# A two-layer hybrid encoder on one core: where the squares are added, when the norm sums run, and the order of the convolution steps

## The chip, the core and the metric

The kernel runs on one core of one Trainium2 chip. The metric is the device time of one execution in microseconds (us). Engines are named as the profile names them: PE (TensorE; PEld are its weight loads), DVE (VectorE), ACT (ScalarE), POOL (GpSimd) and SP (SyncE, which only issues transfers here). "L564" is line 564 of the kernel before.

## The reference, cut to what matters

Two sequences (512 and 256 tokens, together T = 768 columns) go through two layers of width 1024. All arithmetic is float32.

```
for l in range(DEPTH):
    xn = rmsnorm(x, norm1_g[l])
    z = xn @ w_in[l]
    o_a = mixer_a(...)   # gelu, layernorm, spatial gating
    o_b = mixer_b(...)   # banded attention with a sink and a relative bias
    o_c = mixer_c(...)   # q and k: RMS norm, gain, 2-D rotary; full attention
    merged = sum over the mixers of sigmoid(xn @ w_gate + b_gate) * (o @ w_branch)
    x = x + merged @ w_out[l]
    x = x + conv_ffn(rmsnorm(x, norm2_g[l]), w_up[l], conv_w[l], conv_b[l], w_down[l])
return rmsnorm(x, final_g)

def conv_ffn(x, w_up, cw, cb, w_down):
    h = x @ w_up
    hp = jnp.pad(h, ((0, 0), (1, 1), (0, 0)))
    h = hp[:, :-2] * cw[0] + hp[:, 1:-1] * cw[1] + hp[:, 2:] * cw[2] + cb
    gt, val = jnp.split(h, 2, axis=-1)
    return (jax.nn.silu(gt) * val) @ w_down
```

## The kernel before

Activations lie transposed: eight tiles of 128 channels by 768 tokens. Every float32 product is three matmuls, of a high and a low half: wh*xh, wh*xl, wl*xh. ACT makes a weight's high half `wh` (L327, L337), and DVE the low half `wl` (`flush`, L357); DVE or ACT take the results out of PSUM. The program gives each engine its instructions in the order in which they are written; nothing reorders them, so an instruction that waits holds up everything behind it on its engine. A `plan()` lists the weights in order of use. At most three pairs of halves are held, and the next 512 KB weight is loaded by SP only when `flush` has read the raw tile of an earlier one.

**First norm.** The start of the program makes the halves of the eight input tiles (L1275 to L1278, L489, L490) and squares each tile on ACT (`sumsq`, L499). The first product (`dense_tok`, mixer A, L564) runs at the same time, on inputs not yet normed. The squares are added into two sums: tiles 2 to 5 by a POOL-issued transfer that accumulates in SBUF (L508), tiles 6 and 7 and the two sums by DVE (L504, L506). In the middle of the second half of that product PE sums over the channels (`rstd_tok`, L514); then DVE (L517) and POOL (a power of -0.5, L520) make the factor that ACT applies as it empties PSUM (L596).

**Mixer C's tables.** `cs` (cosines and sines) and the gains are fetched by POOL-issued transfers (L880, L885); the gain transfers repeat 64 numbers over 128 partitions and six blocks. DVE multiplies them into `tab` (L888). The product for k and v of mixer C follows (`dense_tok`, L564), then the generator `qknorm`, which uses `tab` (L903).

**FFN.** `layer_out` ends with the last of eight output projections; its squares are summed like those of the start. Then w_up comes in seven pieces for each of 22 groups g, 12 matmuls of 384 columns each, in the order P1, P4 of g-1, P2, P3 of g-1, P6, P5, P7 (the first group: P1, P2, P6, P5, P7). After (0, P5) come `rstd_tok` and `rstd_diag` (DVE L530, ACT L531, DVE L532), after (1, P1) `rstd_bc` (PE L544, ACT L546), whose result scales h in `scaled` (L1066). The transfers `sum1` to `sum4` (POOL, L275) prepare weights for the pieces; each is issued at the start of a piece.

After P4 the value half, after P3 the gate half of a group goes through steps that `later(n, f)` sets n ticks ahead. A piece gives two ticks, a down projection one per k (three or four). `CHAIN` gives the ticks: scaled, centre (ACT, L1058), taps (two DVE instructions, L1062 and L1063), and for the gate half silu (ACT, L1086), the product (DVE, L1089), high half (ACT, L1095), low half (DVE, L1101). The last group uses `CHAIN_END`. The buffer h of group g is written again by group g+2 (first by ACT, L1129, at the end of its P1). Down projections (L435) of a finished chunk lie between the pieces and after them; each fills one of two PSUM tiles `d`, and DVE adds it to x (L1180), or in the last chunk of the last layer (L1170).

Of the kernel before, what the change touches and what calls it, by code (L numbers as in the profile page):

```python
# [13 lines left out]
ALU = mybir.AluOpType  # L14
# [6 lines left out]
KD = D // P  # L21
# [4 lines left out]
HD = 64  # L26
# [4 lines left out]
D_FF = 2816  # L31
NJ = D_FF // P
FFC = [(0, 3), (3, 3), (6, 3), (9, 3), (12, 3), (15, 3), (18, 4)]
CHAIN = (2, 4, 6, 9, 11, 13, 15)
CHAIN_END = (1, 2, 3, 5, 6, 7, 8)
TAIL = 5
HT = T // 2
HW = T + 3
# [36 lines left out]
def ffn_steps(l):  # L75
# [14 lines left out]
    for g, p in seq:  # L90
# [4 lines left out]
        if p == "P3" and ends.get(g, last) < last:  # L95
            ready.append((t + CHAIN[-1] + 2, ends[g]))
        while ready and ready[0][0] <= t:
# [32 lines left out]
def encoder_kernel(ctx, tc, x_d, w_d, vec_d, ln_d, rope_d, gqk_d, oneh_d, relb_d, mask_d, id_d, y_d):  # L130
    nc = tc.nc
    PE, ACT, DVE, POOL = nc.tensor, nc.scalar, nc.vector, nc.gpsimd
# [19 lines left out]
    def page(w=T, dt=F32):  # L152
        return pp.tile([P, w], dt, tag="pg", name=nm("pg"))
# [243 lines left out]
    def start_bg(gen, rate):  # L397
        bg.append((gen, rate))
# [10 lines left out]
    def finish_bg(n=0):  # L409
        while len(bg) > n:  # L410
            if next(bg[0][0], "end") == "end":
                bg.pop(0)
# [38 lines left out]
    st = {}  # L451
# [39 lines left out]
        if k is not None:  # L491
            sumsq(x_ap, k, new=lambda: unit(F32)[:, 0])

    def sumsq(x_ap, k, dve=False, new=None):

        n = x_ap.shape[-1]
        c = 0 if dve else k % 2
        sq = (new or page)()[:, 0:n]
        ACT.activation(sq, x_ap, AF.Square)  # L499
        if k == c:  # L500
            st["acc", c] = sq
            return
        if dve or k >= KD - 2:
            DVE.tensor_tensor(st["acc", 0], st["acc", 0], sq, ALU.add)  # L504
            if not dve and k == KD - 2:
                DVE.tensor_tensor(st["acc", 0], st["acc", 0], st.pop(("acc", 1)), ALU.add)  # L506
        else:
            POOL.dma_start(out=st["acc", c], in_=sq, accum_op=ALU.add)  # L508
# [69 lines left out]
    def layer_mixers(l, xs):  # L578
# [299 lines left out]
        cs = page()  # L878
        for g in range(2):
            POOL.dma_start(out=cs[:, g * 384:(g + 1) * 384], in_=rope_d[g])  # L880
        tab = []
        for g in range(2):
            gt = page()
            for s in range(2):
                POOL.dma_start(  # L885
                    out=gt[:, s * 384:(s + 1) * 384],
                    in_=bass.AP(gqk_d.tensor, gqk_d.offset + ((l * 2 + g) * 2 + s) * HD, [[0, P], [0, NT], [1, HD]]))
            DVE.scalar_tensor_tensor(gt, cs, -(HD ** -0.5) if g == 0 else 1.0, gt, ALU.mult, ALU.mult)  # L888
            tab.append(gt)

        def qknorm(z, nh, tb, cats, dst):
# [65 lines left out]

        dense_tok(("in2", l, 1792 + 512, 0), ("in2", l, 1792 + 512, 1), xs, evac_kv)
        finish_bg()
        start_bg(qknorm(zk, 2, tab[1], "k", kc), BG_N)  # L960
        for c in range(2):
            z = flat(unit(F32))
# [75 lines left out]
    def layer_ffn(l, xs2, x_mid, x_spill):  # L1038
# [14 lines left out]
        def cw(i, ct):  # L1053
            return vec[:, VCW + i * 44 + ct:VCW + i * 44 + ct + 1]
# [3 lines left out]
            ACT.activation(f, h[:, 1:770], AF.Identity, scale=cw(1, ct), bias=vec[:, VCB + ct:VCB + ct + 1])  # L1058
            return f

        def taps(f, h, ct):
            DVE.scalar_tensor_tensor(f, h[:, 0:769], cw(0, ct), f, ALU.mult, ALU.add)  # L1062
            DVE.scalar_tensor_tensor(f, h[:, 2:771], cw(2, ct), f, ALU.mult, ALU.add)  # L1063

        def scaled(h):
            DVE.tensor_tensor(h[:, 1:770], h[:, 1:770], st["bcg"][:, 1:770], ALU.mult)  # L1066

        def conv_v(g):
            s = G[g]
            hv = s["h"][:, 1]  # L1070

            def c():
                s["fv"] = centre(hv, NJ + g)
            for n, f in zip(CHAIN_END if g == NJ - 1 else CHAIN,
                            (lambda: scaled(hv), c, lambda: taps(s["fv"], hv, NJ + g))):
                later(n, f)

        def conv_g(g):
            s = G[g]
            hg = s["h"][:, 0]  # L1080

            def c():
                s["fg"] = centre(hg, g)

            def si():
                ACT.activation(s["fg"], s["fg"], AF.Silu)  # L1086

            def mu():
                DVE.tensor_tensor(s["fg"], s["fg"], s["fv"], ALU.mult)  # L1089

            def hi():
                u = unit()
                f = s["fg"]
                for a, b, o in ((0, 512, 0), (512, 768, 1)):
                    ACT.activation(u[:, 0, a:b], f[:, a + o:b + o], AF.Copy)  # L1095
                s["u"] = u

            def lo():
                u, f = s["u"], s["fg"]
                for a, b, o in ((0, 512, 0), (512, 768, 1)):  # L1100
                    DVE.tensor_tensor(u[:, 1, a:b], f[:, a + o:b + o], fl(u[:, 0, a:b]), ALU.subtract)  # L1101
                hs[g] = u
                del G[g]
            for n, f in zip(CHAIN_END if g == NJ - 1 else CHAIN,
                            (lambda: scaled(hg), c, lambda: taps(s["fg"], hg, g), si, mu, hi, lo)):
                later(n, f)

        RIGHT = ((1 + HT, 513, 0, 512 - HT), (514, 770, 512 - HT, HT))
# [55 lines left out]
        def evac(c, m, cuts, ps):  # L1164
            last = c == len(FFC) - 1
            final_ = last and l == DEPTH - 1
            if final_:
                t0, t1 = cuts
                xa = st["xu"][m // 2][:, m % 2, t0:t1]
                DVE.tensor_tensor(xa, ps[:, 0, 0:t1 - t0], xa, ALU.add)  # L1170
                sumsq(xa, m, dve=True)
                if t0 and m == 2:
                    finish_bg()
                if m == KD - 1:
                    start_bg(final(st["xu"], t0, t1), 1.0)
                    if t0:
                        finish_bg()
                return
            xa = D.pop((c, m))
            DVE.tensor_tensor(h2(xa), ps[:, :, 0:384], h2(xa), ALU.add)  # L1180
            nc.sync.dma_start(out=(x_spill if last else x_mid)[m], in_=xa)
            if last:
                u = unit()
                prep(xa, st["vec"][:, VN1 + m:VN1 + m + 1], u, m)
                xs_next.append(u)
# [5 lines left out]
        for s in steps:  # L1191
            if s[0] == "pc":
                piece(s[1], s[2])
                if (s[1], s[2]) == (0, "P5"):
                    rstd_tok()
                    rstd_diag()
                elif (s[1], s[2]) == (1, "P1"):
                    rstd_bc(gap=True)
                elif s[1] == NJ - 1 and s[2] == "P3":
                    deep = 3  # L1200
                    if l < DEPTH - 1:
                        load_vec(l + 1)
                    else:
                        st["xu"] = [unit(F32) for _ in range(4)]
                continue
            _, c, m, cuts = s
            j0, nj = FFC[c]
            last = c == len(FFC) - 1
            final_ = last and l == DEPTH - 1
            for _, c2, m2, cuts2 in downs[0:deep]:  # L1210
                if not (c2 == len(FFC) - 1 and l == DEPTH - 1):
                    fetch(c2, m2)
                elif cuts2[0] == 0:
                    fetch_last(m2)
            downs.pop(0)
            while any(j not in hs for j in range(j0, j0 + nj)):
                tick()
            if cuts[0] == 0:
                hi, lo = W.get(("down", l, c, m))
                if final_:  # L1220
                    kept[m] = hi, lo
            else:
                hi, lo = kept[m]
            ps = dps()
            dense(ps, hi, lo, 0, [(w, j0 + k) for w, k in kidx(nj)], hs, True, True, cuts=cuts)
            evac(c, m, cuts, ps)
            if m == KD - 1 and not (final_ and cuts[0] == 0):
                for j in range(j0, j0 + nj):
                    del hs[j]
# [24 lines left out]
    with tc.manual_schedule():  # L1254
# [3 lines left out]
        xu = [unit(F32) for _ in range(4)]  # L1258
# [13 lines left out]
        for k in range(KD):  # L1272
            u = unit()
            if k < 4:
                ACT.activation(u[:, 0], xu[k // 2][:, k % 2], AF.Identity, scale=st["vec"][:, VN1 + k:VN1 + k + 1])  # L1275
                parts[k][0]()
                parts[k][1]()
                DVE.scalar_tensor_tensor(u[:, 1], xu[k // 2][:, k % 2], st["vec"][:, VN1 + k:VN1 + k + 1], fl(u[:, 0]),  # L1278
                                         ALU.mult, ALU.subtract)
            else:  # L1280
                prep(xu[k // 2][:, k % 2], st["vec"][:, VN1 + k:VN1 + k + 1], u, None)
            xs.append(u)
            if k == 3:
                W.load()
            if k == 5:
                W.split()
                W.flush()
            if k > 2:
                sumsq(xu[(k - 3) // 2][:, (k - 3) % 2], k - 3)
        for k in range(KD - 3, KD):  # L1290
            sumsq(xu[k // 2][:, k % 2], k)
        del u, xu
        spill = [dram.tile([P, T], F32, name=f"sp{k}") for k in range(KD)]
        x_mid = [dram.tile([P, T], F32, name=f"xm{k}") for k in range(KD)]
# [135 lines left out]
```

## Time and profile before

| | |
|---|---|
| time, median of 3 runs | 2453.21 us (2449.05 to 2453.59) |
| profiled execution | 2457.03 us, span 2455.3 us |
| busy PE / DVE / ACT / POOL | 2388.1 / 1523.8 / 1110.0 / 260.3 us |
| mean granted TensorE clock | 0.989 |
| HBM traffic | 243.93 MB read, 52.43 MB written |

The span runs from the first to the last instruction of the profiled execution; its own time is 1.7 us longer. A row of waits names who ended an engine's idle time, with the sum in us, how often, and the longest. A row of the timeline has its start, its duration, the engine, line and operation, and in brackets the engine's idle time before it and what ended that. Releasers are inferred: where two things ended at once, the row may name the wrong one.

### The profile page before, as it was taken

What the parts mean: (1) busy time and instruction counts of PE and PEld (TensorE: products, weight loads), DVE (VectorE), ACT (ScalarE), POOL (GpSimd) and SP (SyncE); (2) the same over time, 40 slices, a digit from 0 to 9 for tenths busy, and PEclk for the clock granted to TensorE, in tenths of its full rate; (3) what the DMA queues carried; (4) which work ended last, traced back from release to release, by engine and by line L of the source; (5) the groups of instructions that cost most, each with busy time, mean ns of one, the idle gap of its engine ahead of it and who ended that gap; (6) DMA issues with size and microseconds to landing.
All of it is one profiled execution on the core that took longest, in us unless ns stands there. A gap on an engine that the chain in (4) does not pass through costs nothing.

```text
span 2455.3 us, 38491 instructions
## 1 busy us (share of the span) xinstructions
PE 2388.1 (97%) x14990; PEld 2315.9 (94%) x14990; DVE 1523.8 (62%) x2656; ACT 1110.0 (45%) x2184; POOL 260.3 (11%) x390
## 2 busy tenths in 40 slices
PE   7999999999999999999999999999999999999997
PEld 7998999889989999999999999998899899999996
DVE  4555535554558777777645554555445687777785
ACT  4344434662345444444433443456424554444452
POOL 1000110000122111111000000100001211111100
PEclk8999999999999999999999999999999999999998
DMA  5511231012467888887732113210135688888854
GB/s 159 108 52 57 52 64 61 27 35 73 137 161 173 244 225 231 230 228 209 219 108 62 57 50 63 61 45 34 44 102 161 145 221 230 228 230 227 227 160 147
DMA packets 134950, 328.24 MB, mean 134 GB/s; under 512 B 15976, under 2 KB 29416, under 8 KB 134768
## 3 DMA queue, kind: packets, MB, share of 16 engines
q1 hardware_dynamic: 101232, 251.83, 31.6%
q0 software_dynamic: 33536, 73.95, 17.0%
q8 instruction: 118, 1.93, 0.3%
q14 instruction: 64, 0.52, 0.1%
HBM read 243.93 MB, written 52.43 MB: 121 GB/s over the span
## 4 chain that ended last, share of the span: by engine, by line
PE 85%; DMA 5%; DVE 4%; ACT 3%; issue 2%; POOL 0%; SPq 0%; POOLq 0%; DVEq 0%; ACTq 0%
PE d L435 47%; PE ga L1121 12%; PE gb L1121 9%; PE d L564 8%; PE s L809 3%; PE s L796 2%; PE s L757 2%; DMA qc<-w_pk 2%; DMA pg<-gqk 1%; DVE wl L357 1%; PE s L669 1%; ACT wh L327 1%; DMA qd<-qc 1%; DMA raw<-w_pk 1%; DMA pg<-pg 0%
## 5 line engine op out<-in xcount | busy, mean ns | idle before, releaser
L435 PE MATMUL d<-u,wh 128*128 128x384 f32 x4480 | 990.1, 343 | 6.8 <-ACT pg L1086 6.3
L435 PEld LDWEIGHTS d<-u,wh 128*128 128x128 f32 x4480 | 782.6, 189 | 21.8 <-issue 11.0
L435 PE MATMUL d<-u,wl 128*128 128x384 f32 x2240 | 575.3, 338 | 0.0
L435 PEld LDWEIGHTS d<-u,wl 128*128 128x128 f32 x2240 | 408.0, 188 | 0.0
L357 DVE TENSOR_TENSOR wl<-raw,wh 128x512 fp32r<-128x512 f32 (+1 forms) x261 | 248.4, 953 | 232.5 <-ACT wh L337 180.8
L1121 PE MATMUL ga<-u,wh 128*128 128x384 f32 x1408 | 364.5, 340 | 7.6 <-ACT u L1129 4.4
L1121 PE MATMUL gb<-u,wh 128*128 128x384 f32 x1056 | 271.0, 338 | 1.9 <-DVE u L1131 1.9
L1121 PEld LDWEIGHTS ga<-u,wh 128*128 128x128 f32 x1408 | 257.1, 189 | 9.5 <-ACT u L1129 5.0
L564 PE MATMUL d<-wh,u 128*128 128x256 f32 x1344 | 248.3, 285 | 3.0 <-ACT u L596 1.9
L1121 PE MATMUL ga<-u,wl 128*128 128x384 f32 x704 | 238.7, 339 | 0.0
L564 PEld LDWEIGHTS d<-wh,u 128*128 128x128 f32 x1344 | 210.9, 191 | 5.2 <-ACT u L596 3.1
L564 PE MATMUL d<-wl,u 128*128 128x256 f32 x672 | 190.7, 284 | 4.9 <-DVE wl L357 4.8
L1121 PEld LDWEIGHTS gb<-u,wh 128*128 128x128 f32 x1056 | 191.6, 188 | 2.7 <-ACT wh L327 1.8
L337 ACT ACTIVATE wh<-raw 128x1024 fp32r<-128x1024 f32 x129 | 135.3, 1049 | 104.3 <-PE d L564 44.9
L1121 PE MATMUL gb<-u,wl 128*128 128x384 f32 x528 | 178.0, 337 | 0.0
L1058 ACT ACTIVATE pg<-u,vec 128x769 f32<-128x769 f32 x88 | 91.0, 1034 | 124.5 <-DVE u L1066 82.0
L1180 DVE TENSOR_TENSOR pg<-d,pg 128x768 f32<-128x768 f32 x104 | 99.5, 956 | 76.5 <-PE d L435 76.0
L564 PEld LDWEIGHTS d<-wl,u 128*128 128x128 f32 x672 | 128.6, 191 | 5.5 <-DVE wl L357 5.2
L1121 PEld LDWEIGHTS ga<-u,wl 128*128 128x128 f32 x704 | 133.2, 189 | 0.0
L662 DVE TENSOR_TENSOR u<-s,u 128x128 fp32r<-128x128 f32 (+1 forms) x112 | 36.9, 329 | 114.5 <-ACT u L661 114.3
L757 PE MATMUL s<-u,u 128*128 128x256 f32 (+2 forms) x384 | 99.9, 342 | 2.2 <-ACT pg L797 1.6
L768 ACT ACTIVATE pg<-pg,sm 128x257 f32<-128x257 f32 (+1 forms) x96 | 52.5, 547 | 109.1 <-DVE sm L766 104.7
(204 smaller groups left out, 3190.1 us busy)
## 6 DMA issues: line engine op xcount, KB each, us to landing
raw<-w_pk SPq DMA_DIRECT2D x174, 512.0 KB, 3.7
pg<-xm SPq DMA_DIRECT2D x104, 384.0 KB, 4.6
xm<-pg SPq DMA_DIRECT2D x96, 384.0 KB, 3.4
u<-w_pk SPq DMA_DIRECT2D x96, 192.0 KB, 3.6
qa<-w_pk SPq DMA_DIRECT2D x44, 256.0 KB, 3.8
qb<-w_pk SPq DMA_DIRECT2D x44, 256.0 KB, 3.2
qc<-w_pk SPq DMA_DIRECT2D x44, 256.0 KB, 3.2
qd<-w_pk SPq DMA_DIRECT2D x44, 256.0 KB, 3.5
```

The costliest lines, as they stand in the source:

```text
L337: ACT.activation(hi[:, :n], t[:, :n], AF.Copy)
L357: DVE.tensor_tensor(lo, t, fl(hi), ALU.subtract)
L435: PE.matmul(out=ps[:, h, 0:b - a], lhsT=w, rhs=x[:, a:b], start=first and i == 0 and pi == 0, stop=last and i == nk - 1 and pi == 2,)
L564: PE.matmul(out=outs[t], lhsT=x, rhs=w, start=k == 0 and pi == 0 and t % 2 == 0, stop=k == KD - 1 and pi == 2, skip_group_check=True)
L662: DVE.tensor_tensor(u[:, 1, a:b], ps, fl(u[:, 0, a:b]), ALU.subtract)
L757: PE.matmul(out=ps[:, 0:w], lhsT=q, rhs=kb[:, c, lo * P:hi * P], start=c == 0, stop=c == 1)
L768: ACT.activation(lg, lg, AF.Exp, bias=mn, scale=-1.0, accum_out=su)
L796: PE.transpose(ps[:, b * P:(b + 1) * P], lg[:, b * P:(b + 1) * P], ident)
L809: PE.matmul(out=ps[e * HD:(e + 1) * HD, 0:P], lhsT=vtok[:, (lo + b) * P + kv * HD:(lo + b) * P + (kv + 1) * HD], rhs=pT, start=b == 0, sto ...
L1058: ACT.activation(f, h[:, 1:770], AF.Identity, scale=cw(1, ct), bias=vec[:, VCB + ct:VCB + ct + 1])
L1121: PE.matmul(out=o, lhsT=a[:, w], rhs=x[:, b], start=p in ("P1", "P2", "P5") and kp == 0 and pi == 0, stop=kp == 3 and pi == 2, skip_group_ ...
L1180: DVE.tensor_tensor(h2(xa), ps[:, :, 0:384], h2(xa), ALU.add)
```

## The change

Four parts. (1) In the start, `sumsq` takes an engine: one running sum, squares 2 and 4 added by POOL, the others by DVE, and no accumulating transfer. (2) In the FFN, `rstd_tok` and `rstd_diag` come after (0, P6) instead of (0, P5). (3) The two taps become two steps, one tick apart, in the chain of every group; the last group's chain ends at tick ten instead of eight, with its taps at ticks four and five instead of three. (4) The two DVE products that make mixer C's tables come after the product for k and v.

```
-CHAIN = (2, 4, 6, 9, 11, 13, 15)
-CHAIN_END = (1, 2, 3, 5, 6, 7, 8)
+CHAIN = (2, 4, 6, 7, 9, 11, 13, 15)
+CHAIN_END = (1, 2, 4, 5, 6, 8, 9, 10)
...
-    def sumsq(x_ap, k, dve=False, new=None):
+    def sumsq(x_ap, k, eng=None, new=None):
...
-        c = 0 if dve else k % 2
+        c = 0 if eng else k % 2
...
-        if dve or k >= KD - 2:
-            DVE.tensor_tensor(st["acc", 0], st["acc", 0], sq, ALU.add)
-            if not dve and k == KD - 2:
+        if eng or k >= KD - 2:
+            (eng or DVE).tensor_tensor(st["acc", 0], st["acc", 0], sq, ALU.add)
+            if not eng and k == KD - 2:
...
-            DVE.scalar_tensor_tensor(gt, cs, -(HD ** -0.5) if g == 0 else 1.0, gt, ALU.mult, ALU.mult)
             tab.append(gt)
...
         dense_tok(("in2", l, 1792 + 512, 0), ("in2", l, 1792 + 512, 1), xs, evac_kv)
         finish_bg()
+        for g in (1, 0):
+            DVE.scalar_tensor_tensor(tab[g], cs, -(HD ** -0.5) if g == 0 else 1.0, tab[g], ALU.mult, ALU.mult)
         start_bg(qknorm(zk, 2, tab[1], "k", kc), BG_N)
...
-        def taps(f, h, ct):
-            DVE.scalar_tensor_tensor(f, h[:, 0:769], cw(0, ct), f, ALU.mult, ALU.add)
-            DVE.scalar_tensor_tensor(f, h[:, 2:771], cw(2, ct), f, ALU.mult, ALU.add)
+        def tap(f, h, ct, k):
+            DVE.scalar_tensor_tensor(f, h[:, k:769 + k], cw(k, ct), f, ALU.mult, ALU.add)
...
-                            (lambda: scaled(hg), c, lambda: taps(s["fg"], hg, g), si, mu, hi, lo)):
+                            (lambda: scaled(hg), c, lambda: tap(s["fg"], hg, g, 0), lambda: tap(s["fg"], hg, g, 2), si, mu, hi, lo)):
...
-                sumsq(xa, m, dve=True)
+                sumsq(xa, m, DVE)
...
-                if (s[1], s[2]) == (0, "P5"):
+                if (s[1], s[2]) == (0, "P6"):
                     rstd_tok()
                     rstd_diag()
...
             if k > 2:
-                sumsq(xu[(k - 3) // 2][:, (k - 3) % 2], k - 3)
+                sumsq(xu[(k - 3) // 2][:, (k - 3) % 2], k - 3, DVE if k % 2 == 0 else POOL)
         for k in range(KD - 3, KD):
-            sumsq(xu[k // 2][:, k % 2], k)
+            sumsq(xu[k // 2][:, k % 2], k, DVE)
```

The value half's list (`conv_v`) is changed in the same way. The plan of weights and of down projections is as before, since it uses only the last entry of `CHAIN`.

## Rows read from the trace of the kernel before

**Rows 1.** Page, part 1: busy us, share, instructions of each engine.
```profile
PE 2388.1 (97%) x14990; PEld 2315.9 (94%) x14990; DVE 1523.8 (62%) x2656; ACT 1110.0 (45%) x2184; POOL 260.3 (11%) x390
```
**Rows 2.** Waits of PE, whole span: us in total, times, longest.
```profile
PE s L514 <- DVE pg L504: 9.5, 1, 9.5
PE d L435 <- ACT pg L1086: 6.3, 2, 3.2
PE d L564 <- DVE wl L357: 4.8, 2, 3.2
...
PE d L544 <- ACT pg L531: 3.8, 2, 2.9
...
PE ga L1121 <- ACT u L1137: 3.2, 4, 1.1
```
**Rows 3.** Timeline of ACT and of PE in the first 35 us.
```profile
14.93 0.83 ACT L499 ACTIVATE pg<-u 128x768 f32<-128x768 f32 x1
...
18.05 2.30 ACT L499 ACTIVATE pg<-u 128x768 f32<-128x768 f32 x3
...
31.95 2.72 PE L514 MATMUL s<-ones,pg 128*128 128x2 f32 x12 [9.46 <-DVE pg L504]
```
**Rows 4.** The chain that ended last: start, us, what, and how many.
```profile
25.00 4.79 DMA pg<-pg
...
34.67 6.58 PE d L564 x36
...
326.35 17.61 PE d L564 x134
...
552.22 151.43 PE d L435 x864
...
1189.37 41.56 PE d L435 x228
...
1528.16 16.12 PE d L564 x134
```
**Rows 5.** Windows: us, busy PE, PEld, DVE, ACT, POOL; granted clock; DMA.
```profile
32.00:42.00 10.00, 9.24 (x48) 9.03 (x48) 4.08 (x8) 2.29 (x6) 2.92 (x4) 0.63 0.37 114
```
**Rows 6.** Timeline of POOL and of DVE: single instructions.
```profile
334.10 2.54 POOL L908 TENSOR_TENSOR sm<-sm,neghalf 128x12 f32<-128x12 f32 x1 [28.04 <-DVE sm L906]
...
334.99 0.96 DVE L915 TENSOR_TENSOR u<-u,u 128x768 f32<-128x768 f32 x1
...
709.13 0.96 DVE L504 TENSOR_TENSOR pg<-pg,pg 128x768 f32<-128x768 f32 x1 [0.17 <-ACT pg L499]
```
**Rows 7.** Timeline of DVE around mixer C's tables, layer 0.
```profile
324.20 0.96 DVE L888 SCALAR_TENSOR_TENSOR pg<-pg,pg 128x768 f32<-128x768 f32 x1 [3.74 <-DMA pg<-gqk]
...
331.99 0.95 DVE L903 TENSOR_TENSOR u<-pg,pg 128x768 f32<-128x768 f32 x1
```
**Rows 8.** Timeline of POOL and of PE at the FFN's norm, layer 0.
```profile
713.80 0.86 POOL L275 DMA_DIRECT2D qc<-w_pk  x1 [7.24 <-DMA qc<-w_pk]
...
718.80 0.84 POOL L275 DMA_DIRECT2D qd<-qc  x1 [3.28 <-DMA qc<-w_pk]
719.37 1.66 POOL L520 TENSOR_TENSOR sm<-sm,neghalf 128x6 f32<-128x6 f32 x1
...
714.38 1.40 PE L514 MATMUL d<-ones,pg 128*128 128x2 f32 x12
...
722.95 0.80 PE L544 MATMUL d<-pg,onesr 128*128 128x512 f32 x1 [2.88 <-ACT pg L531]
...
728.80 0.60 PE L1121 MATMUL gb<-u,wh 128*128 128x384 f32 x2
```
**Rows 9.** Timeline of ACT in the FFN of layer 0.
```profile
759.47 0.49 ACT L1129 ACTIVATE u<-ga 128x384 f32<-128x384 f32 x1 [1.88 <-DVE pg L1063]
```
**Rows 10.** Timeline of DVE at the end of layer 0's FFN.
```profile
1182.24 1.01 DVE L1062 SCALAR_TENSOR_TENSOR pg<-u,vec,pg 128x769 f32<-128x769 f32 x1
...
1188.28 0.95 DVE L1180 TENSOR_TENSOR pg<-d,pg 128x768 f32<-128x768 f32 x1
```

More of the change, by code (lines that the diff above doesn't have):

```diff
@@ L1074, in conv_v @@
             for n, f in zip(CHAIN_END if g == NJ - 1 else CHAIN,
-                            (lambda: scaled(hv), c, lambda: taps(s["fv"], hv, NJ + g))):
+                            (lambda: scaled(hv), c, lambda: tap(s["fv"], hv, NJ + g, 0), lambda: tap(s["fv"], hv, NJ + g, 2))):
                 later(n, f)
```

## The prediction

> **What bounds the kernel now.** I read the page's busy times first: PE is busy 97% of the span, at nearly full clock [rows 1]. So a saved instruction on another engine is worth nothing by itself; only a wait of PE, and the slow matmuls that follow a long wait, can be won back. The second view is the waits of PE. Its largest rows are the first norm (9.5), the end of both FFNs (6.3 in two), wl in front of L564 (4.8 in two), the FFN's norm (3.8 in two) and L1137 (3.2 in four) [rows 2]: 27.6 us, and the parts of the change point at all five. The third view, the timeline of each engine around each wait, says which instruction PE really waited for. The fourth, the chain, gives the rate behind it: undisturbed, 134 matmuls of L564 take 16.12 us, 0.1203 each, and 864 of L435 151.43, 0.1753 each [rows 4]. After the first norm the granted clock averages 0.63 over 10 us [rows 5]: part of that stretch runs at the lower of the two levels (1.2 GHz), after PE has stood still.
>
> **First norm.** PE reaches the sums of the first norm 9.46 us before 31.95 [rows 3], at 22.5, and the last transfer into the sums alone takes 4.79 from 25.00 [rows 4], with three dependent DVE adds behind it. The change takes out four such transfers and puts in five DVE adds for three and two POOL adds. A DVE add of this form is 0.96 [rows 6]. POOL adding two 128x768 tiles is in no row. From below it costs what DVE takes, 0.96; from above the transfer that it replaces, 4.79; POOL's only tensor-tensor row, a power of 12 columns in 2.54 [rows 6], is about 0.2 a column, which as a far end would make 160 us. I take 2.1, between the two nearest rows as a ratio. The Trainium skill, GPSIMD Engine Reference, section 3.1, has GpSimd 1.96 times slower than VectorE in this add at 2048 columns; that would make 1.9 here by estimate, and the sum 0.2 larger; no run here shows it.
>
> Square 2 stands at 14.93 + 0.83 = 15.76, square 4 near 18.9 [rows 3]. POOL's first add and DVE's add of square 3 end at 15.8 + 2.1 + 1.0 = 18.9, just with square 4. Then come POOL's second add (to 21.0) and three DVE adds of about 1.06 with the handover (to 24.2). So L514 starts near 24.2 instead of 31.95: 7.75. Behind DVE's add of square 3, which waits for POOL, stands the low half of the last input, L490; it moves back by some 0.7, and PE, which needs it, arrives that much later at a wait that is there anyway, about 1 us long. Behind the adds stand also two wl of L357, needed only by the next product. Behind POOL's adds stand its two transfers for the layer norm and the power L520, which is needed later still. If the wait shrinks to 1 us, I expect the clock to stay up, since the 1.6 us wait in front of layer 1's L564 (4.8 less 3.2, [rows 2]) is followed by matmuls at full rate [rows 4]. Then 36 matmuls fall from 6.58 [rows 4] to 36 x 0.1203 = 4.33, and L514 from 2.72 [rows 3] to 1.40 as in the FFN [rows 8]: 2.25 + 1.32. Sum 11.3. With a POOL add of 0.96 PE's arrival decides: about 12.5. With 4.79 both adds lie on the path, 5.4 later: 2.3, without the clock. The part breaks even at 2.1 + 7.75 / 2, about 6 us for one add.
>
> **Mixer C's tables.** DVE stands until 324.20 for the transfer of the gains [rows 7], and the two wl that PE needs are queued behind L888. Without L888 they are made as soon as their high halves are, more than 7 us earlier, and PE's waits in both layers go: 4.8 [rows 2]. Layer 0's stretch then also runs at layer 1's rate: 17.61 - 16.12 = 1.49 [rows 4]. Sum 6.3. L888 in its new place still waits to about 324.2, but now only `qknorm` is queued behind it. L903 started at 331.99 [rows 7], since the wl ahead of it waited for a weight whose load had waited in turn for the late wl. It should now start near 327.2, 4.8 earlier, and PE arrives 4.7 earlier: the same slack. The transfers stay where they are.
>
> **FFN norm.** L514 does not wait now; it follows P5 at 714.38 [rows 8]. One piece earlier is 12 x 0.1753 = 2.1, at 712.3. The last add of squares ends at 709.13 + 0.96 [rows 6], so there is no new wait. What gains is not the 2.1 but POOL's order: L520 at 719.37 stood behind a transfer that waited until 718.80 for the transfer of 713.80 [rows 8]. In its new place it stands behind that of 713.80 alone. It can start near 714.4, 5 us earlier, and the chain from there to PE's L544 (3.58 us, 719.37 to 722.95) ends near 718.0, low halves 718.8; PE arrives at 720.1, and the wait of 2.88 goes. From 722.95 to 728.80 PE did four matmuls of 512 and twelve of 384 columns [rows 8], at full rate 4 x 0.234 + 2.10 = 3.04 instead of 5.85. Layer 0: 2.88 + 2.81 = 5.7. Layer 1: 3.8 - 2.88 = 0.9 [rows 2]; no clock counted. Sum 6.6. L530, L531 and L532 now hold DVE and ACT through P5 and P7; behind them stand wh and wl of (0, P4), due at 721.1, and free to run from 718.8. That costs nothing while the chain is less than some 1.5 us later than I have it.
>
> **Taps.** In the groups before the first down projections PE waits 0.7 to 1.1 for L1137, which ACT has behind L1058, which waits for `scaled`, which DVE has behind both taps. With one tap ahead of it, it comes 1.0 earlier, and these 3.2 go [rows 2]. But the second tap of the gate half moves back, and L1129 already waits 1.88 for it [rows 9]; replaying DVE's queue in the new order I find that tap ending 0.2 later. DVE and ACT pass work round in a ring here, so PE would then wait for P2's evacuation instead. I count 0, from -1.5 to 3. Among the down projections PE never waits: nothing.
>
> **End of the FFN.** The profile names L1086; but the third down projection after the last piece needs the PSUM tile that L1180 empties from 1188.28, to 1189.23, and PE starts at 1189.37 [rows 4, 10]. Ahead of L1180 DVE has the value half's taps (1182.24, 1.01 each), L1066, L1101, and the gate half's taps. With ticks four and five the gate half's taps fall behind L1180, which comes 2.1 earlier. A wait of about 1.0 is left of 3.2, and 0.35 at the next tile, where those taps now lie ahead of L1180. The clock: 228 matmuls take 41.56 [rows 4] for 39.97 at full rate: 1.6. So 3.15 + 1.6 - 1.4 = 3.35 for each FFN, taking the same clock for the second: 6.6 for both. The chain ends two ticks later, but its low half is read only by the fourth k of the first projection of the last chunk, some 1 us after it is made.
>
> **Rivals.** (a) *POOL and DVE shut each other out of SBUF.* Then POOL's two adds and three DVE instructions of about 1 us (the wl, two L490) stand one after the other, the input halves come some 3.5 late, PE slows behind them (about 1.5), and 11.3 becomes 6. Against it: L915, with two SBUF inputs, took 0.96 inside POOL's 2.54 [rows 6]. The Trainium skill, SBUF — State Buffer, section "Who interferes with whom", says that such an instruction contends with a GpSimd instruction reading SBUF; this row does not agree, though the power reads little. With a dear POOL add (4.79: 2.3) this case gives 2429 to 2433. (b) *The FFN's ring absorbs.* The four groups before the first down projections are near the limit of DVE and ACT; if they don't follow PE's start, the 6.6 of the norm are lost, or the split taps cost 0.5 a group: 2429 to 2432. (c) *Tables too late.* If `qknorm` keeps its old time, PE waits at its transposes what it gained: 6.3 lost, 2430. (d) *Slower:* POOL's add priced by the column like its power. The other parts save 19.5, so the whole turns slower when two adds cost 19.5 + 4.9 more than break-even, from 18 us for one add; at 160 the kernel is some 290 slower. For it there is only the power's row; a power is many steps.
>
> **How the numbers follow.** 11.3 + 6.3 + 6.6 + 6.6 = 30.8 from the profiled execution's 2457.0 gives 2426.2. That execution lies 3.8 above the median of the runs; if all of that is waits of the same kind with slower clock, the median loses less, if none, it falls to 2422.4. I take 2424. Chances: the sum as worked out 0.63 (2417 to 2431), (a) 0.14, (b) 0.13, (c) 0.05, (d) 0.02, and 0.03 that several of them leave less than 4.9 us. With POOL at 0.96 and the L1137 waits gone the time is 2419, or 2415 from the lower start; (a) and (b) together give 2437. Range 2414 to 2438. Faster by over 0.2% (4.9 us, about what a measurement of this kernel tells from no change): 0.95; within 0.03; slower 0.02.
>
> **What would show it.** L514 near 24 with a wait of about 1 and the clock at 1.0 after it; POOL's adds near 2 us. No wait on wl at L564, L888 still held to 324. L520 directly behind the transfer of `sum1`, no wait at L544. At the end of both FFNs about 1 us and no slow matmuls. L1137 gone from the waits, perhaps L1131 larger. Wrong would be: L514 after 29, a new wait at the transposes of `qknorm`, or waits in the first groups that grow by what the norm gave.

## The result and the profile after

The changed kernel takes 2441.95 us (median of 4 runs, 2438.26 to 2443.67) against 2453.4 before (4 runs): ratio 0.9945, 95% interval 0.9931 to 0.9959. That is 13.5 us faster, where 2424, that is 29, was forecast; the time lies above the range. The profiled execution of the changed kernel took 2438.26 us (span 2436.5, mean granted clock 0.992); it is the fastest of its runs, and the one of before (2457.03) is slower than all of its own, so sizes below come from ratios of many runs, and the traces say where.

Waits of PE after, whole span (us in total, times, longest):

```profile
PE s L669 <- ACT u L925: 4.1, 1, 4.1
...
PE d L435 <- ACT u L657: 2.9, 1, 2.9
...
PE d L564 <- issue: 2.7, 1, 2.7
...
PE d L564 <- DVE u L490: 2.2, 2, 1.2
...
PE d L435 <- DVE pg L1180: 1.8, 2, 0.9
...
PE ga L1121 <- ACT u L1137: 0.7, 2, 0.4
```

The first norm, the end of the FFNs, the wait for wl and the FFN's norm, the first four rows shown in [rows 2], are gone or down to 1.8 (L1180). The largest row now, L1129 with 4.4 in two, was as large before; [rows 2] does not show it and the prediction passes it over, and no part of the change points at it. Three rows are new or much larger: L669 (the transposes of `qknorm`, layer 1), the wait for nothing visible in L564 (mixer C's first q product, layer 0), and L657 (the key projection of mixer B, layer 0; 0.47 before).

The start, timeline of POOL, DVE and PE after, and the granted clock up to the sums and in the stretch of [rows 5] (in a window's row the clock is the third number from the end, 0.86 and 1.00; DMA share and GB/s follow):

```profile
15.98 2.36 POOL L504 TENSOR_TENSOR pg<-pg,pg 128x768 f32<-128x768 f32 x1 [13.95 <-ACT pg L499]
20.17 2.47 POOL L504 TENSOR_TENSOR pg<-pg,pg 128x768 f32<-128x768 f32 x1 [1.83 <-DVE pg L504]
...
14.49 1.01 DVE L490 SCALAR_TENSOR_TENSOR u<-u,vec,u 128x768 fp32r<-128x768 f32 x1
16.76 2.40 DVE L490 SCALAR_TENSOR_TENSOR u<-u,vec,u 128x768 fp32r<-128x768 f32 x1
19.08 0.95 DVE L504 TENSOR_TENSOR pg<-pg,pg 128x768 f32<-128x768 f32 x1
...
22.68 3.09 DVE L504 TENSOR_TENSOR pg<-pg,pg 128x768 f32<-128x768 f32 x3 [1.72 <-POOL pg L504]
...
25.82 1.50 PE L514 MATMUL s<-ones,pg 128*128 128x2 f32 x12
...
14.00:26.00 12.00, 9.78 (x66) 9.17 (x65) 9.94 (x10) 10.60 (x14) 5.90 (x4) 0.86 0.33 114
...
32.00:42.00 10.00, 9.37 (x78) 9.37 (x79) 2.02 (x3) 2.01 (x4) 0.00 (x0) 1.00 0.18 57
```

L514 starts at 25.82 instead of 31.95 [rows 3], with no wait row, and the clock stays at its upper level after it. Ahead of it, it does not: behind PE's two waits for L490 (0.97 and 1.18 us, ending at 21.01) the granted clock is at the lower level, 0.50, from 22 to 24. PE then comes to the sums just as DVE's last add ends (25.77), so this costs nothing: in n_only below, at 1.00 throughout, PE waits 1.59 and L514 starts at 25.62. POOL's adds take 2.36 and 2.47. The DVE instruction L490 that runs beside the first of them takes 2.40, its neighbour 1.01.

The FFN's norm and the end of the first FFN, timelines of POOL and PE after; they answer to [rows 8] and [rows 10]:

```profile
708.12 0.86 POOL L275 DMA_DIRECT2D qc<-w_pk  x1 [7.21 <-DMA qc<-w_pk]
708.71 1.65 POOL L520 TENSOR_TENSOR sm<-sm,neghalf 128x6 f32<-128x6 f32 x1
...
714.23 0.86 PE L544 MATMUL d<-pg,onesr 128*128 128x512 f32 x4
...
1175.61 0.94 PE L435 MATMUL d<-u,wh 128*128 128x384 f32 x4 [0.92 <-DVE pg L1180]
```

L520 follows its transfer at once, L544 does not wait and runs at full rate (four in 0.86, where one took 0.80), and 0.92 is left of the wait at the end.

Mixer C and the key projection, where the time went. The chain of the changed kernel (start, us, what), then its timelines of ACT, DVE and PE there:

```profile
62.16 23.34 DMA raw<-w_pk
...
301.02 20.87 PE d L564 x176
321.89 2.66 issue
324.56 13.89 PE d L564 x103
...
1496.75 25.90 DMA raw<-w_pk
```
```profile
85.61 1.06 ACT L337 ACTIVATE wh<-raw 128x1024 fp32r<-128x1024 f32 x1 [14.10 <-DMA raw<-w_pk]
...
326.10 1.06 ACT L337 ACTIVATE wh<-raw 128x1024 fp32r<-128x1024 f32 x1 [6.82 <-DMA raw<-w_pk]
...
1522.68 1.07 ACT L337 ACTIVATE wh<-raw 128x1024 fp32r<-128x1024 f32 x1 [9.87 <-DMA raw<-w_pk]
...
325.50 1.83 DVE L960 SCALAR_TENSOR_TENSOR pg<-pg,pg 128x768 f32<-128x768 f32 x2 [13.56 <-DMA pg<-gqk]
...
1521.99 1.83 DVE L960 SCALAR_TENSOR_TENSOR pg<-pg,pg 128x768 f32<-128x768 f32 x2 [16.52 <-DMA pg<-gqk]
...
1531.58 0.75 PE L669 MATMUL s<-identr,u 128*128 128x128 f32 x4 [4.07 <-ACT u L925]
```

Three weight loads of 512 KB take 23 to 26 us, where the median of all 174 is 3.7 (the one of layer 0 has no chain row: from the end of DVE's wl at 303.15 to ACT's start at 326.10). Two of them run beside the four transfers of gains, one beside the 2048 KB transfer that spreads the bias table in DRAM, issued at 52.50 and landed 44.1 us later. That last load was slow before the change too: 20.9 us, beside the same transfer.

### The profile page after: what moved, and what is told of

Same layout as the page of the kernel before. It is cut to its first block, busy times and chain, and to the rows that moved or that the text cites. A ratio compares the mean times of both kernels' runs of the same rounds, so it can differ in the third digit from the quotient of the medians.

```text
span 2436.5 us, 38504 instructions
## 1 busy us (share of the span) xinstructions
PE 2384.4 (98%) x14990; PEld 2312.4 (95%) x14990; DVE 1525.0 (63%) x2658; ACT 1109.4 (46%) x2184; POOL 261.1 (11%) x388
## 4 chain that ended last, share of the span: by engine, by line
PE 86%; DMA 4%; DVE 4%; ACT 3%; issue 3%; POOL 0%; SPq 0%; POOLq 0%; DVEq 0%; ACTq 0%
PE d L435 48%; PE ga L1121 13%; PE gb L1121 9%; PE d L564 7%; PE s L809 3%; PE s L796 2%; PE s L757 2%; DMA raw<-w_pk 2%; DMA qb<-w_pk 1%; DVE wl L357 1%; DMA qc<-w_pk 1%; PE s L669 1%; ACT wh L327 0%; ACT wh L337 0%; DMA qd<-qc 0%
## 5 line engine op out<-in xcount | busy, mean ns | idle before, releaser
L357 DVE TENSOR_TENSOR wl<-raw,wh 128x512 fp32r<-128x512 f32 (+1 forms) x261 | 248.3, 952 | 225.4 <-ACT wh L337 188.7
L564 PE MATMUL d<-wh,u 128*128 128x256 f32 x1344 | 249.5, 286 | 7.0 <-issue 2.7
L564 PEld LDWEIGHTS d<-wh,u 128*128 128x128 f32 x1344 | 211.9, 192 | 9.3 <-ACT u L596 3.1
L564 PE MATMUL d<-wl,u 128*128 128x256 f32 x672 | 190.9, 284 | 0.0
L337 ACT ACTIVATE wh<-raw 128x1024 fp32r<-128x1024 f32 x129 | 135.3, 1050 | 114.9 <-PE d L564 33.2
L1063 DVE SCALAR_TENSOR_TENSOR pg<-u,vec,pg 128x769 f32<-128x769 f32 x176 | 179.0, 1017 | 2.1
L1180 DVE TENSOR_TENSOR pg<-d,pg 128x768 f32<-128x768 f32 x104 | 99.4, 956 | 70.6 <-PE d L435 70.0
L564 PEld LDWEIGHTS d<-wl,u 128*128 128x128 f32 x672 | 129.0, 192 | 0.0
```

What stands on the lines that cost most here:

```text
L337: ACT.activation(hi[:, :n], t[:, :n], AF.Copy)
L357: DVE.tensor_tensor(lo, t, fl(hi), ALU.subtract)
L564: PE.matmul(out=outs[t], lhsT=x, rhs=w, start=k == 0 and pi == 0 and t % 2 == 0, stop=k == KD - 1 and pi == 2, skip_group_check=True)
L1063: DVE.scalar_tensor_tensor(f, h[:, k:769 + k], cw(k, ct), f, ALU.mult, ALU.add)
```

## The experiments

**Theories.** T1: L888 in its old place was a brake. It held the two wl of L357, and the weight load that may start only when wl has read the raw tile, until the gains had landed; without it load and gains run at once and both crawl. T2: the earlier first norm pushes a weight load's use ahead of its end, since that load runs beside the transfer of the bias table. T3: POOL's adds and DVE shut each other out. The rival of each stands in its expectation. Each kernel was timed in rounds beside the kernel before on the same chip; the table gives ratios to that one. A thousandth is 2.5 us, so two ratios have to differ by some 0.002, 5 us, to be told apart.

| kernel | us, median | before beside it | ratio, 95% interval |
|---|---|---|---|
| changed | 2441.95 | 2453.40 | 0.9945 (0.9931 to 0.9959) |
| t_old | 2436.50 | 2455.83 | 0.9920 (0.9907 to 0.9933) |
| t_only | 2460.50 | 2455.83 | 1.0021 (1.0008 to 1.0034) |
| t_held | 2428.24 | 2455.83 | 0.9899 (0.9883 to 0.9915) |
| t_wide | 2429.45 | 2455.83 | 0.9896 (0.9881 to 0.9910) |
| n_only | 2447.99 | 2453.18 | 0.9980 (0.9969 to 0.9991) |
| n_dve | 2438.32 | 2453.18 | 0.9940 (0.9923 to 0.9957) |
| b_late | 2443.64 | 2453.18 | 0.9959 (0.9943 to 0.9974) |
| f_only | 2447.22 | 2453.18 | 0.9972 (0.9959 to 0.9985) |
| taps_only | 2456.85 | 2456.58 | 1.0004 (0.9993 to 1.0016) |
| e_old | 2447.86 | 2456.58 | 0.9973 (0.9962 to 0.9983) |
| b_hop | 2437.56 | 2456.58 | 0.9922 (0.9909 to 0.9935) |
| best | 2423.07 | 2456.58 | 0.9864 (0.9850 to 0.9879) |

**t_old: the tables alone undone**

```
+            DVE.scalar_tensor_tensor(gt, cs, -(HD ** -0.5) if g == 0 else 1.0, gt, ALU.mult, ALU.mult)
             tab.append(gt)
...
-        for g in (1, 0):
-            DVE.scalar_tensor_tensor(tab[g], cs, -(HD ** -0.5) if g == 0 else 1.0, tab[g], ALU.mult, ALU.mult)
```

> The changed kernel with the two gain products put back beside their loads (mixer C tables as before, all else as changed). Theory T1 (a traffic jam): the gain product used to hold VectorE's split remainder, and with it the next 512 KB weight load, until the gains had landed; without it load and gains run at once, the load takes 23 to 26 us instead of about 4, and the products behind it pay 4.5 us over both layers more than the wait that went. T1 expects about 4.5 us faster than the changed kernel (2437), TensorE's waits for the split remainder (3.2 and 1.6 us) back, the weight load there at about 4 us, and no wait at the transposes in layer 1. Rival R1 (moving the products is worth the 6.3 us predicted, and the loss came from elsewhere): about 6 us slower than the changed kernel (2448).

It is faster than the changed kernel: 0.9945 - 0.9920 of 2453 is 6.1 us (the intervals just touch). Its timeline of DVE and ACT in layer 0, and of ACT in layer 1:

```profile
318.86 0.96 DVE L888 SCALAR_TENSOR_TENSOR pg<-pg,pg 128x768 f32<-128x768 f32 x1 [2.03 <-DMA pg<-gqk]
319.73 2.35 DVE L357 TENSOR_TENSOR wl<-raw,wh 128x1024 fp32r<-128x1024 f32 x2
...
324.57 1.06 ACT L337 ACTIVATE wh<-raw 128x1024 fp32r<-128x1024 f32 x1 [5.05 <-DMA raw<-w_pk]
...
1517.03 1.06 ACT L337 ACTIVATE wh<-raw 128x1024 fp32r<-128x1024 f32 x1 [3.81 <-DMA raw<-w_pk]
```

The load is issued when the first wl has read its tile, near 321.0, and is there 3.6 us later. PE waits for wl again, 3.8 us in two, but neither at L669 nor for nothing visible. R1 falls.

**t_only: the tables alone moved**

```
-            DVE.scalar_tensor_tensor(gt, cs, -(HD ** -0.5) if g == 0 else 1.0, gt, ALU.mult, ALU.mult)
             tab.append(gt)
...
+        for g in (1, 0):
+            DVE.scalar_tensor_tensor(tab[g], cs, -(HD ** -0.5) if g == 0 else 1.0, tab[g], ALU.mult, ALU.mult)
```

> The kernel before with the two gain products moved and nothing else. T1: not faster; from equal to 5 us slower than before (2453 to 2458), weight load of 20 us or more beside the gains. R1: about 6 us faster (2447).

1.0021: 5 us slower than before, the slow end of what T1 had, and against R1, which had it 6 us faster. The same step costs 5 to 6 us in either direction. Timeline of ACT in layer 1 and the chain:

```profile
1540.73 1.06 ACT L337 ACTIVATE wh<-raw 128x1024 fp32r<-128x1024 f32 x1 [10.57 <-DMA raw<-w_pk]
```
```profile
1532.85 5.76 issue
1538.61 6.48 PE d L564 x43
```

**t_held: the load kept back until the tables are made**

```
-                if then:
+                if then and self.hold:
+                    self.held += 1
+                elif then:
                     then()
...
+        W.hold = True
         dense_tok(("in2", l, 1792 + 512, 0), ("in2", l, 1792 + 512, 1), xs, evac_kv)
...
+        for s in (0, 1):
+            DVE.tensor_copy(small(2)[:, 0:1], W.rawt["in2", l, 1792, s][:, 0:1])
+        W.hold = False
+        for _ in range(W.held):
+            W.load()
```

> The changed kernel, with the weight load behind the key/value product's split held until the gain products are done (two one-column copies on VectorE keep the old tile occupied; nothing else is changed). T1: load and gains are apart again, the gains land some 20 us after their issue instead of 26 to 31, TensorE's waits in the first query product (2.7 us) and at the transposes of layer 1 (4.0 us) shrink, and the time is 3 to 9 us below the changed kernel (2433 to 2439). R1 or another cause: both waits stay and the time is equal or longer, since the weight load now starts later.

0.9899: 11 us below the changed kernel, more than expected. The load of layer 0 starts later than in the changed kernel (behind the two small copies, at 318.4 instead of 303.15) and ends sooner. Timeline of DVE and ACT in layer 0:

```profile
316.46 1.82 DVE L965 SCALAR_TENSOR_TENSOR pg<-pg,pg 128x768 f32<-128x768 f32 x2 [4.77 <-DMA pg<-gqk]
...
323.71 1.06 ACT L339 ACTIVATE wh<-raw 128x1024 fp32r<-128x1024 f32 x1 [4.67 <-DMA raw<-w_pk]
```

The gains land by 316.46 instead of 325.50, though nothing was done to them: from the issue of the first to L888's product 19 us in layer 0 and 20 in layer 1, where the changed kernel has 28 and 31. All of PE's waits there are gone but one of 0.5. This is the experiment that shows T1: the same transfers, only kept apart.

**t_wide: the gains in rows of 1536 bytes**

```
-  ... gqk_d.offset + ((l * 2 + g) * 2 + s) * HD, [[0, P], [0, NT], [1, HD]]
+  ... gqk_d.offset + ((l * 2 + g) * 2 + s) * NT * HD, [[0, P], [1, NT * HD]]
-        "gqk": np.array(gq, np.float32),
+        "gqk": np.tile(np.array(gq, np.float32), NT),
```

> The changed kernel with the gains laid out in memory six times over, so that one transfer reads rows of 1536 bytes instead of six pieces of 256 bytes at a time (same bytes landed, same values). T1 with the small pieces as its cause: gains land within 5 us of issue instead of 20 to 31, the weight load beside them takes 4 to 6 us, both waits go, and the time is about 11 us below the changed kernel (2431). If the small pieces are not what slows the load: the load stays above 15 us and the time near 2442.

0.9896: 12 us below the changed kernel. The page's list of transfers (last number: median us from issue to landing), DVE and ACT in layer 0, and the chain there:

```profile
pg<-gqk POOLq DMA_DIRECT2D x8, 192.0 KB, 3.9
```
```profile
312.29 1.82 DVE L960 SCALAR_TENSOR_TENSOR pg<-pg,pg 128x768 f32<-128x768 f32 x2
...
319.59 1.07 ACT L337 ACTIVATE wh<-raw 128x1024 fp32r<-128x1024 f32 x1
```
```profile
301.46 33.09 PE d L564 x279
```

The same bytes land in 3.9 us (changed kernel: 19.7), neither instruction waits for a transfer, and the 279 matmuls that took 20.87 + 2.66 + 13.89 = 37.42 take 33.09. The load that wl releases takes 3.7 us. Against t_old, 0.9920 becomes 0.9896, 5.9 us, near the 6.3 that the move was to bring; but t_wide has the widened gains as well, which would help t_old too, so how much of it is the move's is not shown.

**n_only and f_only: one part each on the kernel before**

n_only has `sumsq` as changed and, in the start:

```
-                sumsq(xu[(k - 3) // 2][:, (k - 3) % 2], k - 3)
+                sumsq(xu[(k - 3) // 2][:, (k - 3) % 2], k - 3, DVE if k % 2 == 0 else POOL)
         for k in range(KD - 3, KD):
-            sumsq(xu[k // 2][:, k % 2], k)
+            sumsq(xu[k // 2][:, k % 2], k, DVE)
```

> The kernel before with the first norm's sum alone changed (VectorE and GpSimd add the squares). Theory T2: the first product starts 9 to 10 us sooner, but the weight load issued near 62 us then falls into the transfer of the bias table (2048 KB) and gives 3 to 4 us back where TensorE waits for the split at L657, so 5 to 7 us faster than before remain. Rival (the sum as predicted, nothing given back): 11 us faster.

f_only:

```
-                if (s[1], s[2]) == (0, "P5"):
+                if (s[1], s[2]) == (0, "P6"):
```

> The kernel before with the FFN norm's sums made one piece sooner and nothing else. As predicted: 5.7 us in layer 0 and 0.9 in layer 1, 6 to 8 us faster than before, TensorE's waits at L544 gone. Rival (the earlier sums delay the piece before): 0 to 3 us.

f_only: 0.9972, 6.9 us, where 6.6 was forecast; its waits have no L544 on tile `d`. n_only: 0.9980, 4.9 us. Timeline of ACT in n_only:

```profile
85.61 1.06 ACT L337 ACTIVATE wh<-raw 128x1024 fp32r<-128x1024 f32 x1 [14.34 <-DMA raw<-w_pk]
```

The product behind L514 runs 9.2 us sooner than before (29.08 for 38.30 at the same matmul), and by the key projection 9.8 us are won. There PE waits 3.1 for L657, which ACT has behind that L337, and goes on with slower matmuls (0.32 us each for a while, 0.18 in the kernel before); behind them 5.6 us are left (93.90 for 99.47 at the same matmul), and 6.2 from 130 us on. T2's place and size fit, but not all of its reason: load and table were side by side before as well, and both are issued sooner with PE. What differs is that the load takes 23.6 us instead of 20.9; why, no run shows. Near 185 a further 1.4 us goes at a granted clock of 0.50 that the profiled execution of before does not have there. f_only, whose start is that of before, loses as much there, so it is no part of T2.

**n_dve: no additions on POOL**

```
-                sumsq(xu[(k - 3) // 2][:, (k - 3) % 2], k - 3, DVE if k % 2 == 0 else POOL)
+                sumsq(xu[(k - 3) // 2][:, (k - 3) % 2], k - 3, DVE)
```

> The changed kernel with all of the first norm's early additions on VectorE and none on GpSimd. Theory T3 (the two engines shut each other out): every token-scaling copy at L490 takes 1.01 us again instead of up to 2.40, TensorE's waits there (0.97 and 1.18 us) go, the sum's matmul starts at 24 to 25 us instead of 25.8, and the time is 1 to 3 us below the changed kernel. Rival (VectorE has the more work, and GpSimd's help was worth it): the matmul starts later than 25.8 and the time is 0 to 2 us above.

Ratio 0.9940, not to be told from the changed kernel's 0.9945. Timeline of DVE and PE:

```profile
17.72 1.01 DVE L490 SCALAR_TENSOR_TENSOR u<-u,vec,u 128x768 fp32r<-128x768 f32 x1
...
20.59 0.51 PE L564 MATMUL d<-wh,u 128*128 128x256 f32 x2 [1.18 <-DVE u L490]
...
25.17 1.40 PE L514 MATMUL s<-ones,pg 128*128 128x2 f32 x12
```

The lock is real and its price small: every L490 takes 1.01 again, and DVE, which now makes all the adds itself, ends the last at 24.59 instead of 25.77. L514 comes only 0.65 sooner, since PE is late: its granted clock is at 0.50 from 22 to 24 here too. Of the two waits at L490 one falls from 0.97 to 0.29 and the other stays. T3 is right on the mechanism; its price is about 1 us, which the times do not tell from nothing.

**b_late and b_hop: the bias table**

b_late writes the 2048 KB transfer behind the u products:

```
-        POOL.dma_start(out=td, in_=tb[0:8, :].unsqueeze(1).broadcast_to([8, P, 512]))
...
+        if l == 0:
+            table_out()
         kt = proj(("in", l, 1024 + 512))
```

> The changed kernel with the transfer of the bias table (2048 KB, DRAM) issued after the u products instead of ahead of them, so that the weight load issued near 62 us has the DMA engines to itself. Theory T2: this load takes 4 to 6 us instead of 23, TensorE's wait of 2.9 us at the product of the key projection goes, and 3 to 4 us are gained (about 2438), unless the table then comes too late for the first biased attention (VectorE reads it at 152 us). Rival (the load is slow for another reason): it stays above 12 us and nothing is gained.

b_hop leaves it where it is, and reads it from DRAM:

```
+        t1 = dram.tile([8, 512], F32, name="tab1")
+        POOL.dma_start(out=t1, in_=tb[0:8, :])
         td = dram.tile([8, P, 512], F32, name="tab")
-        POOL.dma_start(out=td, in_=tb[0:8, :].unsqueeze(1).broadcast_to([8, P, 512]))
+        POOL.dma_start(out=td, in_=bass.AP(t1.tensor, t1.offset, [[512, 8], [0, P], [1, 512]]))
```

> The changed kernel with the bias table spread to its 128 copies from a 16 KB copy in DRAM instead of from 8 partitions of SBUF (one more small transfer; the same bytes land). Theory T2: if reading 8 partitions is what makes this transfer take 44 us, it takes 8 to 20 us here, is over before the weight load issued near 62 us, this load takes 4 to 8 us, TensorE's wait of 2.9 us behind L657 goes, and 3 to 4 us are gained (2438). Rival (2048 KB in pieces of 2 KB take their time wherever they are read): still 40 us and more, nothing gained.

b_late tested nothing: POOL has no work between the two places that waits for PE, so it issued the transfer only 3.4 us later. Timeline of POOL, and of ACT at the load:

```profile
55.85 1.19 POOL L476 DMA_DIRECT2D tab<-pg  x1
...
85.55 1.06 ACT L337 ACTIVATE wh<-raw 128x1024 fp32r<-128x1024 f32 x1 [13.78 <-DMA raw<-w_pk]
```

b_hop took the transfer itself on. The page's list of transfers, and ACT at the same load:

```profile
tab<-tab POOLq DMA_DIRECT2D x1, 2048.0 KB, 14.6
```
```profile
80.90 1.06 ACT L337 ACTIVATE wh<-raw 128x1024 fp32r<-128x1024 f32 x1 [6.08 <-issue]
```

44.1 us became 14.6. The weight load, issued while the table was still under way, takes 6.9 us instead of 23.3, ACT no longer waits for it, PE has no wait row from 60 to 130 us, and the ratio falls from 0.9945 to 0.9922, 5.6 us (intervals just overlap; 3 to 4 expected). That the table's transfer is what makes the load slow holds. The profiled execution of b_hop lost some 3 us elsewhere: behind PE's wait of 1.60 for the sums the granted clock fell to 0.50, and L514's twelve matmuls took 2.46 (1.50 in the changed kernel).

**taps_only and e_old: the convolution's steps**

taps_only is the kernel before with `tap` as changed and

```
-CHAIN = (2, 4, 6, 9, 11, 13, 15)
-CHAIN_END = (1, 2, 3, 5, 6, 7, 8)
+CHAIN = (2, 4, 6, 7, 9, 11, 13, 15)
+CHAIN_END = (1, 2, 3, 3, 5, 6, 7, 8)
```

> The kernel before with the two taps of each convolution as steps of their own, the last pair's chain at its old ticks. As predicted: nothing (-1.5 to 3 us, a gain being positive), TensorE's waits for the gate's upper parts at L1137 (3.2 us in 4) shorter, the end of both FFNs as before. Rival: the shorter VectorE stretches matter and 3 us or more are gained.

e_old is the changed kernel with

```
-CHAIN_END = (1, 2, 4, 5, 6, 8, 9, 10)
+CHAIN_END = (1, 2, 3, 3, 5, 6, 7, 8)
```

> The changed kernel with the last pair's chain at the old ticks (1, 2, 3, 3, 5, 6, 7, 8) and the taps still steps of their own. As predicted, the ten-tick chain is worth 3.35 us in each layer: 6 to 7 us above the changed kernel, TensorE's waits of 3.2 us each at the start of the down product back in both layers. Rival (the stretch of the chain was worth nothing by itself, the split taps did it): equal to the changed kernel.

taps_only: 1.0004, nothing. e_old: 0.9973, 6.9 us above the changed kernel. Its waits of PE:

```profile
PE d L435 <- ACT pg L1086: 6.3, 2, 3.2
```

All of the gain at the end of the FFN is the ticks'.

**best: the changed kernel with t_wide, n_dve and b_hop together**

> The changed kernel with three edits: gains in rows of 1536 bytes, the first norm's additions all on VectorE, the bias table spread from DRAM. If the three losses are separate, as T1 to T3 have it: 11 + 1 + 3.6 below the changed kernel, about 2426, and no wait of TensorE over 2 us ahead of the first FFN but in the attention. If the table's spread does not shorten: about 2429.

2423.07 us, ratio 0.9864: 33 us below the kernel before and 20 below the changed one, more than the sum of 15.6 expected, and near the sum of what the three brought one by one (12, 1 and 5.6). From 60 to 130 us and around mixer C in both layers PE has no wait but one of 0.5 in the attention. It is the fastest kernel of the study.

## Why the prediction was wrong

Part by part, from the ratios times 2453 us (a gain is positive; by its interval each is uncertain by some 3 us, those from two ratios by some 4 to 5):

| part | forecast | measured | from |
|---|---|---|---|
| first norm | 11.3 | 4.9 | n_only |
| mixer C's tables | 6.3 | -5.2; -6.1 | t_only; t_old |
| FFN norm | 6.6 | 6.9 | f_only |
| taps | 0 | -1.0 | taps_only |
| end of the FFN | 6.6 | 6.9 | e_old |
| sum | 30.8 | 12.5 | measured together 13.5 |

**The step that failed** is one sentence under mixer C's tables: "The transfers stay where they are." The gains' transfers did, in their order. But the wl that were to come 7 us earlier also release a raw tile, and with it a 512 KB load, which the prediction itself had seen two sentences on ("a weight whose load had waited in turn for the late wl"). It took the earlier load as a gain and did not ask what it meets. It met the gains; it took 23 and 26 us instead of 3.6, and the gains came 9 and 11 us later than when kept apart. The wait for wl went, as forecast, in both layers; what was paid is the 2.66 in layer 0, 4.07 at L669 in layer 1, and slow matmuls behind each. Set side by side matmul by matmul, the profiled executions of before and after show both: the part first wins 5.0 us in layer 0 and 1.9 in layer 1, 6.9 where 6.3 was forecast, and then loses 4.3 and 6.9. In t_held and t_wide the same 6.9 are won, and 0.9 and nothing lost. Rival (c), tables too late, and the prediction's own sign of being wrong, a new wait at the transposes of `qknorm`, named the right place in layer 1; but (c) took the tables' old time for the worst.

**First norm, mis-sized.** Up to L514 it went nearly as worked out: 25.82 for 24.2. POOL's adds took 2.36 and 2.47 for 2.1, and the first locked L490 out, so that DVE's add of square 3 ended at 20.03 instead of 18.9: rival (a) came true in one instruction of three, at about 1.1 us. The lock went the other way too: both adds began while a DVE instruction with two SBUF inputs ran (L357 to 16.63, L490 to 20.96), and ended about 1.7 us behind it (1.68 to 1.72 in all eight kernels that have these adds). By estimate from that, an add left alone takes about 1.7, and the 2.1 was too dear, not too cheap; what was missed is the waiting. The Trainium skill, SBUF — State Buffer, section "Who interferes with whom", says that a DVE instruction with two SBUF inputs contends with a GpSimd one that reads SBUF; 2.40 instead of 1.01 agrees with it, where the prediction had set L915's 0.96 [rows 6] against it. In n_only the clock stayed up, and by 29 us 9.2 of the 11.3 had come. That it would stay up was partly luck: behind the same wait of 1.6 us it fell in the profiled execution of b_hop, which cost some 3 us there. What was left out is the next limit: PE now reaches the key projection before a weight that is loaded beside the bias table. In the kernel before, the same load landed just ahead of its use (0.47 us of wait), so there was no slack for a load that takes 2.7 us longer; of 9.8 us won, 5.6 passed (n_only). b_hop takes the limit away. The rest of the way from there to the 4.9 of the ratio lies within its interval.

**FFN norm, taps, end of the FFN: right,** in place, and in size as far as these times can tell. L520 runs at 708.71 right behind its transfer; L544's wait is gone; the waits for L1137 fell from 3.2 to 0.7 and brought nothing; 0.92 us of wait is left at L1180, forecast 1.0. Rival (b), the ring absorbing the norm's gain, did not happen.

**Left open.** The waits for nothing visible in PE's L564 (2.7 in the changed kernel, 5.8 in t_only, 5.4 in b_late and in b_hop, 3.0 in e_old, 1.2 in n_dve) stand in the waits of all six kernels in which load and narrow gains overlap, and in none of the other eight. That ties them to the jam, and makes its price vary from kernel to kernel. What PE lacked no row of the waits says, but the DMA packets point to it: in each of the six, a 16 KB packet on the queue that the profile calls "instruction" ends 1.2 to 1.5 us before PE goes on (changed kernel: packet from 322.29 to 323.25, PE on at 324.56), and the changed kernel and b_hop stop at the same matmul. The packet itself is no slower than others (0.96, median 0.93). So PE seems to have run out of instructions, whose transfer began late in the jam; no run tests this.

## What to carry to other kernels

An instruction that waits is also a brake on everything queued behind it, transfers included: before it is moved out of the way, follow what the freed work will issue, and what that will run beside. A gain early in the program can be lost again at the next load that lands just in time; look for waits of a few tenths of a microsecond behind a transfer, there is no slack there. A transfer in small pieces, or one out of few partitions, can cost nothing while nothing waits behind it, and much beside a load that something waits for: widen it, read it from elsewhere, or keep the two apart.

## What the runs showed of the hardware

- The gains, 192 KB each in pieces of 256 bytes, landed in 16 to 21 us (median), in rows of 1536 bytes in 3.9. The Trainium skill, DMA: Bandwidth & Descriptors, section "Why small descriptors are slow (HBM only)", puts the bus overhead of a 256-byte piece at 27%. The whole transfer differs here by a factor of four to five, so that overhead alone does not account for it; whether the size of the pieces does, or that the same 256 bytes are read six times over, was not separated.
- Beside them, a 512 KB load took 23 to 26 us in the changed kernel instead of 3.6, and the four of a layer took 28 to 31 us from the first issue to the product that waits for the last of them, instead of 19 to 22: both lose when they overlap.
- A 2048 KB transfer into DRAM took 44.1 us out of 8 partitions of SBUF, and 14.6 out of a 16 KB copy in DRAM; a 512 KB load beside it took 23.3 and 6.9.
- A POOL add of two 128x768 tiles took 2.36 to 2.49 us where DVE takes 0.95. Each began inside a DVE instruction with two SBUF inputs and ended 1.68 to 1.72 after that one's end; about 1.7 for the add alone is an estimate from this.
- The granted clock near the first norm differed between profiled executions with the same instructions there: behind a wait of about 1.6 us for the sums it stayed at 1.00 in n_only and fell to 0.50 in b_hop.
